# Seven block products for the MLP's up and gate projections, its rows kept in DRAM, and a down projection by halves of the tokens

## The chip, the cores and the metric

The kernel runs on one core of a Trainium2 chip. The metric is device time, in microseconds (us), from one execution to the next run of the same program. The core has five engines, each with its own queue of instructions: TensorE (PE), VectorE (DVE), ScalarE (ACT), GpSimd (POOL) and SyncE (SP), which here issues the DMA transfers. Engines wait for each other through semaphores. PE's operands come from the on-chip memory SBUF and its sums go to the small memory PSUM.

## What is computed

The reference is one layer of an encoder trunk, for 1024 tokens (S) of width 1024 (D), in float32. The change concerns its last part, the MLP, and the output projection of cross attention just before it:

```python
def conv_glu_ffn(h, w_up, conv_w, conv_b, w_down):
    u = dwconv(h @ w_up, conv_w) + conv_b.astype(h.dtype)   # 3 taps along the tokens
    gate, up = jnp.split(u, 2, axis=-1)                     # 2816 columns each
    return (jax.nn.silu(gate) * up) @ w_down
...
        x = x + cross_attention(rms_norm(x, xa_norm[l]), rms_norm(mem, xa_mem_norm[l]),
                                xa_w_q[l], xa_w_kv[l], xa_w_o[l])
        x = x + conv_glu_ffn(rms_norm(x, ffn_norm[l]), ffn_w_up[l], ffn_conv_w[l], ffn_conv_b[l], ffn_w_down[l])
    return rms_norm(x, final_norm)
```

## The kernel before

**Products in three passes.** Activations lie transposed: 128 features on partitions, tokens along the free axis, eight tiles (KD) for the width. A float32 product is made of three: each operand is split into a high part (fp32r) and the rest, and hi x hi, hi x lo, lo x hi are added in PSUM. `K.split` (L140, L142) makes the two parts: ACT copies to `wh`, then POOL (for weights) or DVE (for activations) subtracts into `wl`. A projection `K.proj` gives 128 output rows for all 1024 tokens: eight 128x128 weight blocks, three passes, two halves of 512 tokens, 48 matmuls of 128x512 (L171). Its sum takes one of two PSUM buffers `pp` of 128x1024. Weights come in two pieces of 128x512 floats (256 KB, tile `wr`), in three buffers.

**Into the MLP.** The eight projections of `wo` add to the residual X, which stays in SBUF as eight tiles of 128x1024. `K.residual` applies the norm's gain and splits into `hf` (tile `big`). The norm's factor of each token (`rrow`) is not applied there; it multiplies the projections' results. Its sum over features is a set of small fp32 matmuls (L229 `colsum`, L221 `rows`).

**The MLP.** `ffn` has 22 tiles f of 128 gate rows and 128 up rows. For each f it runs two projections (96 matmuls); DVE takes each out of PSUM times `rrow` (`ut`, L1396), ACT (L203) and DVE (L189, two steps) do the convolution into `c0` and `c1`, ACT the silu (L1398), DVE the product, and ACT and DVE split it into `g`. After every group of four f, `down` (L1412) multiplies the group before it by the down weights: for each of the eight output tiles up to 96 matmuls, added to X. The last two f are done by halves of the tokens (`part`, L1424), so that the first half's final norm runs beside the second half's matmuls.

**What sets the order.** PE's order is that of the program. The other engines' orders are set by a scheduler from the program's dependences, but for DVE's in `part`, which is written out. A tile's buffer is free for its next writer once all readers of the whole tile before are done.

## Time and profile before

| what | us |
|---|---|
| median of three runs | 2501.03 (2498.71 to 2503.26) |
| span of the profiled execution, first to last instruction | 2497.7 |
| PE busy, sum over the span | 2405.6 |
| first matmul of the up projections starts | 1752.86 |
| last matmul of all starts | 2477.64 |

The profile gives, for one execution, what each engine did and when. "Busy" is time in an instruction; a wait is idle time, put down to the instruction that released it. The chain of waits starts at the last instruction and goes back, at each step, to what the instruction waited for; what lies on it sets the time. The granted clock is the share of 2.4 GHz at which PE was allowed to run.

### The profile page before, as it was taken

What the parts mean: (1) busy time and instruction counts of PE and PEld (TensorE: products, weight loads), DVE (VectorE), ACT (ScalarE), POOL (GpSimd) and SP (SyncE); (2) the same over time, 40 slices, a digit from 0 to 9 for tenths busy, and PEclk for the clock granted to TensorE, in tenths of its full rate; (3) what the DMA queues carried; (4) which work ended last, traced back from release to release, by engine and by line L of the source; (5) the groups of instructions that cost most, each with busy time, mean ns of one, the idle gap of its engine ahead of it and who ended that gap; (6) DMA issues with size and microseconds to landing.
All of it is one profiled execution on the core that took longest, in us unless ns stands there. A gap on an engine that the chain in (4) does not pass through costs nothing.

```text
span 2497.7 us, 31082 instructions
## 1 busy us (share of the span) xinstructions
PE 2405.6 (96%) x11750; PEld 1967.1 (79%) x11750; DVE 1397.0 (56%) x2752; ACT 817.4 (33%) x1201; POOL 733.6 (29%) x515
## 2 busy tenths in 40 slices
PE   7999988999999999999999999999999999999997
PEld 6777667778877778786878888888888888888885
DVE  6883998835938658476445633363444243424345
ACT  6362435534224223241231232253333131313123
POOL 6422224525225233241122222202222222222223
PEclk9999999999999999998999999999999999999998
DMA  7443112432111211112264452121111111111112
GB/s 261 112 108 99 38 59 79 129 122 73 61 47 52 72 51 63 48 51 68 86 251 145 134 168 93 43 81 47 47 47 51 47 51 47 51 47 51 47 47 98
DMA packets 112870, 204.25 MB, mean 82 GB/s; under 512 B 12752, under 2 KB 40400, under 8 KB 112592
## 3 DMA queue, kind: packets, MB, share of 16 engines
q1 hardware_dynamic: 112720, 202.26, 24.5%
q8 instruction: 93, 1.52, 0.3%
q14 instruction: 57, 0.47, 0.1%
HBM read 158.17 MB, written 41.94 MB: 80 GB/s over the span
## 4 chain that ended last, share of the span: by engine, by line
PE 72%; DVE 5%; ACT 1%; DMA 1%; POOL 0%; issue 0%; DVEq 0%; SPq 0%; ACTq 0%
PE pp L171 55%; PE pp L1412 9%; PE sm L1105 3%; DVE w L189 1%; PE sm L1315 1%; DVE y L192 1%; PE pp L1424 1%; DVE rb L1031 1%; DVE t L192 1%; PE sm L1047 1%; PE sm L229 0%; PE sm L1061 0%; PE sm L904 0%; PE sm L1092 0%; PE sm L1076 0%; DMA yraw<-yd 0%
## 5 line engine op out<-in xcount | busy, mean ns | idle before, releaser
L171 PE MATMUL pp<-big,wh 128*128 128x512 f32 x3968 | 1105.6, 398 | 16.2 <-DVE sa L192 12.5
L142 POOL TENSOR_TENSOR wl<-wr,wh 128x512 fp32r<-128x512 f32 (+1 forms) x385 | 536.7, 1397 | 1526.2 <-ACT wh L140 1381.5
L171 PEld LDWEIGHTS pp<-big,wh 128*128 128x128 f32 x3968 | 738.7, 190 | 173.7 <-DVE sa L192 14.8
L140 ACT ACTIVATE wh<-wr 128x512 fp32r<-128x512 f32 (+1 forms) x404 | 250.1, 622 | 1213.9 <-PE pp L171 759.3
L171 PE MATMUL pp<-big,wl 128*128 128x512 f32 x1984 | 623.5, 396 | 0.0
L171 PEld LDWEIGHTS pp<-big,wl 128*128 128x128 f32 x1984 | 370.0, 189 | 75.4
L192 DVE TENSOR_TENSOR X<-X,pp 128x1024 f32<-128x1024 f32 (+1 forms) x72 | 79.2, 1101 | 229.3 <-PE pp L1412 129.7
L1412 PE MATMUL pp<-g,wh 128*128 128x512 f32 x640 | 171.0, 389 | 0.0
L192 DVE TENSOR_TENSOR ut<-pp,rrow 128x1024 f32<-128x1024 f32 x44 | 53.9, 1224 | 203.1 <-PE pp L171 199.2
L189 DVE SCALAR_TENSOR_TENSOR c<-ut,vec,c 128x1023 f32<-128x1023 f32 x88 | 113.0, 1284 | 60.6 <-ACT c L203 59.0
L171 PE MATMUL pp<-yhl,wh 128*128 128x512 f32 x512 | 137.4, 390 | 3.3 <-DVE acc L189 2.1
L1412 PEld LDWEIGHTS pp<-g,wh 128*128 128x128 f32 x640 | 120.2, 188 | 24.9
L171 PE MATMUL pp<-bigq,wh 128*128 128x512 f32 x512 | 137.6, 390 | 0.0
L171 PEld LDWEIGHTS pp<-yhl,wh 128*128 128x128 f32 x512 | 95.9, 188 | 24.4 <-DVE acc L189 2.5
L171 PEld LDWEIGHTS pp<-bigq,wh 128*128 128x128 f32 x512 | 95.9, 188 | 20.7 <-DVE bigq L192 0.4
L1412 PE MATMUL pp<-g,wl 128*128 128x512 f32 x320 | 98.5, 389 | 0.0
L171 PE MATMUL pp<-bigq,wl 128*128 128x512 f32 x256 | 78.9, 389 | 0.0
L171 PE MATMUL pp<-yhl,wl 128*128 128x512 f32 x256 | 78.8, 389 | 0.0
L192 DVE TENSOR_TENSOR y<-y,t 128x8 f32<-128x8 f32 (+30 forms) x248 | 77.9, 353 | 0.0
L192 DVE TENSOR_TENSOR t<-rb,x 128x8 f32<-128x8 f32 (+30 forms) x248 | 77.6, 351 | 0.0
L203 ACT ACTIVATE c<-ut,vec 128x1024 f32<-128x1024 f32 x44 | 54.7, 1244 | 46.9 <-DVE ut L192 46.9
L1412 PEld LDWEIGHTS pp<-g,wl 128*128 128x128 f32 x320 | 60.1, 188 | 12.5
(369 smaller groups left out, 2952.1 us busy)
## 6 DMA issues: line engine op xcount, KB each, us to landing
wr<-in_wi SPq DMA_DIRECT2D x144, 256.0 KB, 2.8
wr<-in_wup SPq DMA_DIRECT2D x88, 256.0 KB, 2.7
thd<-tho SPq DMA_DIRECT2D x32, 512.0 KB, 2.9
thi<-thd SPq DMA_DIRECT2D x32, 512.0 KB, 4.0
wr<-in_wdn SPq DMA_DIRECT2D x40, 256.0 KB, 2.6
wr<-in_wkv SPq DMA_DIRECT2D x32, 256.0 KB, 3.6
X<-in_x SPq DMA_DIRECT2D x16, 512.0 KB, 5.3
wr<-in_wbr SPq DMA_DIRECT2D x32, 256.0 KB, 2.8
```

Of the source, the lines that this page charges most:

```text
L140: self.nc.scalar.activation(hi, src, AF.Copy)
L142: e.tensor_tensor(lo, src, hi.bitcast(F32), SUB)
L171: self.nc.tensor.matmul(ps[:, o:o + step], w[:, i], r[:, k, o:o + step], start=first, stop=last)
L189: self.nc.vector.scalar_tensor_tensor(out, in0, s, in1, op0, op1)
L192: (eng or self.nc.vector).tensor_tensor(out, a, b, op)
L203: self.nc.scalar.activation(out, src, AF.Identity, bias=bias, scale=taps[:, left:left + 1])
L1031: nc.vector.stream_shuffle(rb[:, u, s], y[:, u, s], [j] * 32)
L1047: nc.tensor.matmul(p1[:, i], E[:, i, 0:64], y[:, i], start=True, stop=True)
L1105: mm = lambda out, a, b: nc.tensor.matmul(out, a, b, start=True, stop=True)
L1315: nc.tensor.matmul(ps, qt[:, x, d, c], kT[:, y, d], start=k == 0 and i == 0, stop=k == 1 and i == 2)
L1412: nc.tensor.matmul(ps[:, o:o + 512], w[:, i], g[:, x, o:o + 512], start=i == 0 and q == 0, stop=i == n - 1 and q == 2)
L1424: nc.tensor.matmul(ps, w[:, i], g[:, x, c], start=i == 0 and k == 0, stop=i == n - 1 and k == 2)
```

## The change

**Seven products.** For each f the gate and up blocks (two row blocks) by the two halves of the width (A11, A12, A21, A22) are multiplied with the two halves of the width by the two halves of the tokens (B11 to B22). Instead of eight block products of 12 matmuls (128x512 each) there are seven, with sums of blocks as operands (class `Seven`). The sums on the right, B12-B11 and so on, are made once, beside the `wo` projections, and split into seven operands of four tiles: three in `big`, four in the new tiles t0 to t3. The sums on the left are four DVE operations per f; seven pieces are split per f instead of four. The seven results are combined when they are read from PSUM: product 0 to `p1` (ACT), 1 to `u2`, 3 to `u3`, and 2, 4, 5, 6 to the four quarters of the two `ut` tiles (`ready`), where the row factor is applied on DVE or, for all of ut1, on POOL. Products 0 to 3 and 5 take the halves a and b of one `pp` buffer in turn, 4 and 6 half of the other.

**Room for it.** X no longer stays in SBUF: each tile is read, added to, and stored to DRAM (`x2d`). The right operands need a common scale, so they take the factor of the norm before (`rrow` of attention), and its reciprocal is kept (`rcol`) to undo it. The MLP's product goes to DRAM as well (`gd`).

**Down by halves.** `down` starts after the last f: for each half of the tokens the 22 tiles are read back and split into a ring of 24 slots, which the seven operands held before; output tiles go in pairs, each with all 22 f (132 matmuls), so the weights are loaded twice. X comes back from `x2d` at the end of a pair.

```diff
+class Seven:
...
+    def weights(self, s0, s1, m=4):
...
+        a11 = load(s0[:, 0:m])
+        yield self.parts(a11, m)
+        a21, a22 = load(s1[:, 0:m]), load(s1[:, m:2 * m])
+        x1, x2 = self.raw(m), self.raw(m)
+        K.tt(x1, a21, a22, ADD)
+        K.tt(x2, x1, a11, SUB)
+        yield self.parts(x2, m)
+        a12 = load(s0[:, m:2 * m])
+        yield self.parts(a12, m)
+        K.tt(a21, a11, a21, SUB)
+        yield self.parts(a21, m)
+        yield self.parts(x1, m)
+        yield self.parts(a22, m)
+        K.tt(x2, a12, x2, SUB)
+        yield self.parts(x2, m)
...
+    def run(self, s0, s1, x, pool, ready, m=4):
...
+        ab = K.pp.tile([P, S], F32, name="pp")
+        a, b = ab[:, 0:512], ab[:, 512:S]
+        c = None
+        sm = lambda n: pool[n].tile([P, 512], F32, name=n)
+        for n, ps in enumerate((a, b, a, b, c, b, c)):
+            if n == 4:
+                c = K.pp.tile([P, S], F32, name="pp")[:, 0:512]
+            ps = c if ps is None else ps
+            K.run(self.product(ps, next(w), lambda i: x[n][i], n in (0, 1, 4)))
+            if n == 0:
+                p1 = sm("p1")
+                nc.scalar.activation(p1, a, AF.Copy)
+            elif n == 1:
+                u2 = sm("u2")
+                K.tt(u2, b, p1, ADD)
+            elif n == 2:
+                yield
+                ready(0, 0, a, None)
+                continue
+            elif n == 3:
+                u3 = sm("u3")
+                K.tt(u3, b, p1, ADD)
+            elif n == 4:
+                ready(1, 1, c, u3)
+            elif n == 5:
+                ready(1, 0, b, p1)
+            else:
+                ready(0, 1, c, u2)
+            yield
...
+def ffn(K, tc, big, bq, ot, keep, rrow, rcol, x1d, out):
...
+    for j in (0, 4, 1, 5, 2, 6, 3, 7):
+        x = xr.tile([P, S], F32, name="X")
+        nc.sync.dma_start(x, x1d[j])
+        ps = K.run(K.proj(a["wo"][j], ot[:, 0], ot[:, 1]))
+        K.tt(x, x, ps, ADD)
+        nc.sync.dma_start(x2d[j], x)
+        K.stt(g32[:, j], x, K.v("ffnn", j), rrow, MUL, MUL)
+        K.sumsq(xr, x, S, acc)
...
+    for f in range(NFF):
+        def ready(i, h, ps, add):
+            t, c = ts[i], slice(512 * h, 512 * h + 512)
+            if add is None:
+                K.tt(t[:, c], ps, box["row"][:, c], MUL)
+                return
+            K.tt(t[:, c], ps, add, ADD)
+            if i == 0:
+                K.tt(t[:, c], t[:, c], box["row"][:, c], MUL)
+            elif h == 0:
+                K.tt(t, t, box["row"], MUL, nc.gpsimd)
...
+        nc.scalar.activation(c[0], c[0], AF.Silu)
+        K.tt(c[0], c[0], c[1], MUL)
+        nc.sync.dma_start(gd[f], c[0])
...
+    ff.__exit__(None, None, None)
+    fd = right.enter_context(tc.tile_pool(name="fd", bufs=3, side="right"))
+    more = [K.wp, fd] * 3
+    down(K, gp, fd, gd, x2d, ring, X, more, out)
...
+def down(K, gp, fd, gd, x2d, ring, X, pools, out):
...
+        for j0 in range(0, KD, 2):
+            ps = K.pp.tile([P, S], F32, name="pp")
+            w = 0
+            for f0 in range(0, NFF, 4):
+                n = min(4, NFF - f0)
+                ws = []
+                for j in (j0, j0 + 1):
+                    ws.append(K.weights(a["wdn"][j][:, f0:f0 + n], n, pools[w % len(pools)])[0]())
+                    w += 1
...
+                x = X[q][:, j]
+                nc.sync.dma_start(x, x2d[j, :, c])
+                K.tt(x, x, ps[:, 512 * b:512 * b + 512], ADD)
```

On PE, where one projection ends and the next begins in the up stretch, before (`pp_14754` and `pp_14820` are two buffers):

```order
L171 MATMUL pp_14754<-big_13488,wh_14786 128x512 x4
L171 MATMUL pp_14754<-big_13488,wl_14787 128x512 x2
L171 MATMUL pp_14820<-big_13488,wh_14822 128x512 [waits DVE_49,Activation_49]
L171 MATMUL pp_14820<-big_13488,wh_14822 128x512 x3
L171 MATMUL pp_14820<-big_13488,wl_14823 128x512 [waits Pool_49]
```

And now, from product 0 to product 1 of an f (both in `pp_14924`, halves a and b):

```order
L1433 MATMUL pp_14924<-big_13497,wh_14927 128x512 x2
L1433 MATMUL pp_14924<-big_13497,wl_14928 128x512
L1433 MATMUL pp_14924<-big_13497,wh_14953 128x512 [waits Activation_49]
L1433 MATMUL pp_14924<-big_13497,wh_14953 128x512
L1433 MATMUL pp_14924<-big_13497,wl_14954 128x512 [waits Pool_49]
```

The first matmul of product 1 waits for ACT, with the copy of product 0 out of the same buffer; before, the wait at that place was for the buffer two projections back.

On ACT, in the same stretch, before (`wh` are weight splits):

```order
L140 ACTIVATE g_14610<-c0_14474 128x1024
L140 ACTIVATE wh_14756<-wr_14755 128x512
L203 ACTIVATE c0_14613<-ut_14676,vec_71 128x1024
L140 ACTIVATE wh_14786<-wr_14785 128x512
L1398 ACTIVATE c0_14613<-c0_14613 128x1024
L140 ACTIVATE wh_14822<-wr_14821 128x512
L203 ACTIVATE c1_14614<-ut_14742,vec_71 128x1024
L140 ACTIVATE wh_14852<-wr_14851 128x512
```

And now, from the end of one f (`c1_14914`, `c0_14913`) to the copy `p1_14943` of the next:

```order
L140 ACTIVATE wh_14993<-wr_14945 128x512 [waits PE_49,Pool_49]
L140 ACTIVATE wh_15012<-wr_14949 128x512 [waits PE_49,Pool_49]
L203 ACTIVATE c1_14914<-ut_14819,vec_71 128x1024 [waits Pool_49]
L203 ACTIVATE c0_14913<-ut_14818,vec_71 128x1024 [waits DMAHW6_49,DVE_49]
L140 ACTIVATE wh_15029<-wr_14947 128x512 [waits DMAHW4_49,PE_49,Activation_49]
L1453 ACTIVATE p1_14943<-pp_14924 128x512 [waits PE_49]
L1565 ACTIVATE c0_14913<-c0_14913 128x1024 [waits DVE_49,Activation_49]
L140 ACTIVATE wh_15048<-wr_14950 128x512 [waits PE_49]
```

The two convolutions of one f, the second of them behind the first, now stand ahead of the copy that PE's product 1 waits for; the first waits for POOL.

On DVE, before, around one product c0 x c1:

```order
L192 TENSOR_TENSOR ut_14742<-pp_14681,rrow_14111 128x1024
L189 SCALAR_TENSOR_TENSOR c1_14614<-ut_14742,vec_71,c1_14614 128x1023 x2
L192 TENSOR_TENSOR c0_14613<-c0_14613,c1_14614 128x1024
L142 TENSOR_TENSOR g_14749<-c0_14613,g_14749 128x1024
L192 TENSOR_TENSOR ut_14815<-pp_14754,rrow_14111 128x1024
L189 SCALAR_TENSOR_TENSOR c0_14752<-ut_14815,vec_71,c0_14752 128x1023 x2
L192 TENSOR_TENSOR ut_14881<-pp_14820,rrow_14111 128x1024
```

And now, from the second half of ut0 of one f to product 2 of the next:

```order
L192 TENSOR_TENSOR ut_14818<-pp_14858,u2_14816 128x512 [waits PE_49]
L192 TENSOR_TENSOR ut_14818<-ut_14818,rrow_14190 128x512 [waits DVE_49]
L189 SCALAR_TENSOR_TENSOR c1_14914<-ut_14819,vec_71,c1_14914 128x1023 [waits Activation_49]
L189 SCALAR_TENSOR_TENSOR c0_14913<-ut_14818,vec_71,c0_14913 128x1023 [waits DMAHW6_49,Activation_49]
L189 SCALAR_TENSOR_TENSOR c1_14914<-ut_14819,vec_71,c1_14914 128x1023 [waits DVE_49]
L189 SCALAR_TENSOR_TENSOR c0_14913<-ut_14818,vec_71,c0_14913 128x1023 [waits DVE_49]
L192 TENSOR_TENSOR c0_14913<-c0_14913,c1_14914 128x1024 [waits Activation_49]
L192 TENSOR_TENSOR u2_14969<-pp_14924,p1_14943 128x512 [waits PE_49]
L192 TENSOR_TENSOR ut_14971<-pp_14924,rrow_14190 128x512 [waits PE_49]
```

The convolution steps and here also the gate product, which waits for the silu, stand ahead of `u2_14969`, which PE's product 2 waits for; in 11 of the 21 passages `u2` comes ahead of the gate product.

On SP, where the up projections began to give way to down weights, before:

```order
L152 DMA wr_15063<-in_wup 128x512
L152 DMA wr_15099<-in_wup 128x512
L152 DMA wr_15129<-in_wup 128x512
L152 DMA wr_15169<-in_wdn 128x512
L152 DMA wr_15201<-in_wdn 128x512
```

And now, at the end of the last f (`c0_17514`):

```order
L1626 DMA t1_17525<-x2d_13492 128x512 x4
L1626 DMA t2_17526<-x2d_13492 128x512 x8
L1567 DMA gd_13493<-c0_17514 128x1024
L1602 DMA gr_17615<-gd_13493 128x512
L152 DMA wr_17626<-in_wdn 128x512
L152 DMA wr_17662<-in_wdn 128x512
L152 DMA wr_17698<-in_wdn 128x512
L1602 DMA gr_18478<-gd_13493 128x512
```

The weights `wr_17626` for the second output tile of the first pair stand behind the store of the last f's product and its read back. Their space is that of `c0`, `c1` and `ut`.

## Rows read from the trace of the kernel before

**Rows 1.** The page: busy us (share of the span) xinstructions.

```profile
PE 2405.6 (96%) x11750; PEld 1967.1 (79%) x11750; DVE 1397.0 (56%) x2752; ACT 817.4 (33%) x1201; POOL 733.6 (29%) x515
```

**Rows 2.** Chain of waits, MLP: start us, length us, engine, tile, line, count.

```profile
1767.42 163.25 PE pp L171 x720
...
1974.19 87.04 PE pp L171 x384
```

**Rows 3.** Windows: us, each engine's busy us (x instructions), PEclk, DMA share, GB/s.

```profile
1900.00:2100.00 200.00, 200.00 (x884) 165.68 (x883) 76.00 (x61) 48.72 (x60) 49.22 (x37) 1.00 0.16 49
```

**Rows 4.** Groups by form, 1740 to 2478: xcount, busy us, mean ns, idle.

```profile
L192 DVE TENSOR_TENSOR ut<-pp,rrow 128x1024 f32<-128x1024 f32 x44 | 53.9, 1224 | 203.1 <-PE pp L171 199.2 <-ACT rrow L278 3.9
L189 DVE SCALAR_TENSOR_TENSOR c<-ut,vec,c 128x1023 f32<-128x1023 f32 x88 | 113.0, 1284 | 60.6 <-ACT c L203 59.0
L192 DVE TENSOR_TENSOR X<-X,pp 128x512 f32<-128x512 f32 x15 | 10.1, 681 | 3.4 <-PE pp L1424 3.3
L140 ACT ACTIVATE wh<-wr 128x512 fp32r<-128x512 f32 x128 | 80.9, 632 | 443.0 <-PE pp L171 206.1 <-PE pp L1412 154.2 <-issue 82.8
L203 ACT ACTIVATE c<-ut,vec 128x1024 f32<-128x1024 f32 x44 | 54.7, 1244 | 46.9 <-DVE ut L192 46.9
L1398 ACT ACTIVATE c<-c 128x1024 f32<-128x1024 f32 x22 | 23.1, 1048 | 0.0
L142 POOL TENSOR_TENSOR wl<-wr,wh 128x512 fp32r<-128x512 f32 x128 | 175.1, 1368 | 521.9 <-ACT wh L140 521.9
```

**Rows 5.** Groups by form on POOL, whole span: products of 128x1024.

```profile
L142 POOL TENSOR_TENSOR H<-cm,H 128x1024 fp32r<-128x1024 f32 x4 | 11.2, 2798 | 14.7 <-ACT H L140 14.5
L192 POOL TENSOR_TENSOR Bn<-gcr,g_gh 128x1024 fp32r<-128x1024 f32 x4 | 7.6, 1897 | 5.8 <-PE sm L1076 3.8 <-DVE gcr L825 2.1
```

**Rows 6.** Timeline near the end: start us, length us, engine, instruction, [idle <-releaser].

```profile
2455.54 0.40 PE L1424 MATMUL pp<-g,wl 128*128 128x512 f32 x1
2455.98 0.69 DVE L192 TENSOR_TENSOR X<-X,pp 128x512 f32<-128x512 f32 x1 [0.99 <-PE pp L1424]
...
2467.02 0.69 DVE L192 TENSOR_TENSOR sqa<-sqa,hn 128x512 f32<-128x512 f32 x1 [0.70 <-ACT hn L1429]
2467.77 0.97 PEld L229 LDWEIGHTS sm<-ones,sqa 128*128 128x128 f32 x8 [0.90 <-DVE sqa L192]
```

**Rows 7.** Timeline, one POOL operation beside one of DVE.

```profile
1783.56 1.23 DVE L192 TENSOR_TENSOR c<-c,c 128x1024 f32<-128x1024 f32 x1
...
1784.13 1.82 POOL L142 TENSOR_TENSOR wl<-wr,wh 128x512 fp32r<-128x512 f32 x1 [4.14 <-ACT wh L140]
```

**Rows 8.** Timeline of PE after idle time, and windows that follow such restarts.

```profile
296.92 2.08 PE L171 MATMUL pp<-big,wh 128*128 128x512 f32 x4 [4.42 <-DVE sa L192]
485.63 0.73 PE L171 MATMUL pp<-big,wh 128*128 128x512 f32 x2 [1.79 <-DVE sb L192]
1266.86 1.21 PE L171 MATMUL pp<-yhl,wh 128*128 128x512 f32 x4 [2.11 <-DVE acc L189]
...
296.90:302.00 5.10, 5.08 (x12) 4.06 (x13) 4.75 (x15) 4.63 (x4) 0.00 (x0) 0.50 0.00 0
486.00:491.00 5.00, 5.00 (x16) 3.93 (x15) 2.03 (x2) 2.90 (x4) 3.54 (x2) 0.66 0.28 53
1267.00:1272.00 5.00, 5.00 (x22) 4.10 (x23) 2.89 (x2) 0.43 (x1) 1.30 (x1) 1.00 0.91 320
```

**Rows 9.** The page: DMA issues, count, KB each, median us to landing.

```profile
wr<-in_wup SPq DMA_DIRECT2D x88, 256.0 KB, 2.7
thd<-tho SPq DMA_DIRECT2D x32, 512.0 KB, 2.9
thi<-thd SPq DMA_DIRECT2D x32, 512.0 KB, 4.0
```

**Rows 10.** Timeline: the last matmul of all.

```profile
2477.64 0.39 PE L1424 MATMUL pp<-g,wl 128*128 128x512 f32 x1
```

**Rows 11.** Timeline: the first matmuls of the up projections.

```profile
1752.86 1.07 PE L171 MATMUL pp<-big,wh 128*128 128x512 f32 x4
```

More of the change, by code (lines that the diff above doesn't have):

```diff
@@ L209, in conv, with rows @@
                 self.stt(out[:, :n - s], src[:, s:], taps[:, j:j + 1], out[:, :n - s], MUL, ADD)
-    def rows(self, pool, col, nt, gp=False):
-        dg = pool.tile([P, 8, P], F32, name="dg", bufs=1)[:, :nt]
-        self.tt(dg, self.ident.unsqueeze(1).to_broadcast([P, nt, P]), col.unsqueeze(2).to_broadcast([P, nt, P]), MUL,
-                self.nc.gpsimd if gp else None)
+    def rows(self, pool, col, nt, name="dg"):
+        dg = pool.tile([P, max(nt, 4), P], F32, name=name, bufs=1)[:, :nt]
+        self.tt(dg, self.ident.unsqueeze(1).to_broadcast([P, nt, P]), col.unsqueeze(2).to_broadcast([P, nt, P]), MUL)
         f = dg.rearrange("p a b -> p (a b)")
@@ L270, in gained, with rrow @@
         self.sumsq(pool, x, x.shape[-1], accs)
-    def rrow(self, pool, keep, acc, n=S):
+    def rrow(self, pool, keep, acc, n=S, over=None):
         r = self.rstd(pool, self.colsum(acc, n // P), 1.0 / D, EPS)
+        if over is not None:
+            self.nc.vector.reciprocal(over, r)
         yield
@@ L1279, in memory, with queries @@
         yield
-def queries(K, xr, hx, qt, acc, ahead):
-    rr = K.rrow(xr, xr, acc)
+def queries(K, xr, hx, qt, acc, ahead, keep, rcol):
+    rr = K.rrow(xr, keep, acc, over=rcol)
     row = None
@@ L1299, in queries @@
         K.split(qt[:, 0, i], qt[:, 1, i], t, "dve")
+    return row
 UNITS = [(h, t) for h in range(4) for t in range(8)]
@@ new lines, with __init__, raw, parts @@
+class Seven:
+    def __init__(self, K, raws, sets):
+        self.K, self.raws, self.sets = K, raws, sets
+        self.n = [0, 0]
+    def raw(self, m):
+        self.n[0] += 1
+        pool = self.raws[self.n[0] % len(self.raws)]
+        return pool.tile([P, 4, P], F32, name="wr", bufs=3)[:, :m]
+    def parts(self, src, m):
+        self.n[1] += 1
+        pool = self.sets[self.n[1] % len(self.sets)]
+        n = self.sets.count(pool)
+        wh = pool.tile([P, 4, P], F32R, name="wh", bufs=n)[:, :m]
+        wl = pool.tile([P, 4, P], F32R, name="wl", bufs=n)[:, :m]
+        self.K.split(wh, wl, src, "pool")
+        return wh, wl
+    def weights(self, s0, s1, m=4):
+        K = self.K
+        def load(s):
+            t = self.raw(m)
+            K.nc.sync.dma_start(t, s)
+            return t
+        a11 = load(s0[:, 0:m])
[13 more added lines that the diff above has]
+        yield self.parts(x2, m)
+    def product(self, ps, w, x, first):
+        wh, wl = w
+        m = wh.shape[1]
+        for i in range(m):
+            xh, xl = x(i)
+            for j, (a, b) in enumerate(((wh, xh), (wh, xl), (wl, xh))):
+                self.K.nc.tensor.matmul(ps, a[:, i], b, start=first and i == 0 and j == 0,
+                                         stop=i == m - 1 and j == 2, skip_group_check=not first)
+            yield
+    def run(self, s0, s1, x, pool, ready, m=4):
+        K, nc = self.K, self.K.nc
+        w = self.weights(s0, s1, m)
+        ab = K.pp.tile([P, S], F32, name="pp")
[26 more added lines that the diff above has]
+                ready(0, 1, c, u2)
+            yield
@@ L1525, in tile_trunk @@
     x1d = K.dram.tile([KD, P, S], F32, name="x1d")
-    right = ExitStack()
-    with tc.tile_pool(name="bq", bufs=1) as bq:
+    bs = ExitStack()
+    with tc.tile_pool(name="keep", bufs=1, side="right") as keep:
+        bq = bs.enter_context(tc.tile_pool(name="bq", bufs=1))
+        rcol = keep.tile([P, 8], F32, name="rcol")
         with tc.tile_pool(name="at", bufs=1) as at:
@@ L1544, in tile_trunk @@
                 es = {}
-                queries(K, xr, hx, qt, acc[0], lambda: es.update({n: scores(K, at, qt, kT, n) for n in range(AHEAD)}))
+                rrow = queries(K, xr, hx, qt, acc[0],
+                               lambda: es.update({n: scores(K, at, qt, kT, n) for n in range(AHEAD)}), keep, rcol)
             with tc.tile_pool(name="att", bufs=1) as p:
@@ L1548, in tile_trunk @@
                 attend(K, p, at, qt, ot, kT, vt, es)
-        xr = right.enter_context(tc.tile_pool(name="xr2", bufs=1, side="right"))
-        X = xr.tile([P, KD, S], F32, name="X")
-        hf = big.tile([P, 2, KD, S], F32R, name="big")
-        acc = []
-        for j in range(KD):
-            nc.sync.dma_start(X[:, j], x1d[j])
-            ps = K.run(K.proj(a["wo"][j], ot[:, 0], ot[:, 1]))
-            K.residual(xr, X[:, j], ps, j, "ffnn", hf[:, 0], hf[:, 1], acc)
-    ffn(K, X, hf, acc[0], xr, out)
-    right.close()
+        ffn(K, tc, big, bs, ot, keep, rrow, rcol, x1d, out)
 def kernel(**inputs):
```

196 lines of the change are left out of this document (113 added, 83 removed).

## The prediction

> **What bounds the kernel now.** I read the page first: TensorE (PE) is busy 96% of the span [rows 1]. The chain of waits then tells how it runs through the MLP: stretches of hundreds of matmuls with nothing between them [rows 2]. 163.25 / 720 and 87.04 / 384 both give 0.2267 us from one matmul to the next. One f (one pair of 128 gate and 128 up rows) is 96 of them, 21.76 us. The windows over this stretch show PE 100% busy at granted clock 1.00, VectorE (DVE) 38% and ScalarE (ACT) 24% [rows 3]. So matmuls taken out are time gained there, as long as whatever replaces them keeps PE fed.
>
> **What is removed.** Seven products of 12 matmuls are 84 instead of 96 per f: 12 x 0.2267 x 22 = 59.8 us less if PE stays full, 19.04 us per f. The down projection keeps its 1056 matmuls (239.4 us).
>
> **What is added, as totals.** Per f, from [rows 4]: DVE had two ut multiplies and a g split of the same shape (1.22), four convolution steps (1.28) and the gate product (1.23, [rows 7]): 10.0 us. It now has eleven operations of 512 (0.68, the X row): six out of PSUM, one multiply by the row factor, four weight combinations; with the same steps and product 13.9. ACT goes from some 7 to 8.6 (seven wh and p1 at 0.63, two convolutions at 1.24, silu 1.05). GpSimd (POOL) goes from four wl (1.37) to seven plus the multiply of ut1 by the row, 128x1024. The trace has that shape on POOL at 1.90 to 2.80 [rows 5]; two whole operands are nearest the upper row, so 2.8, 12.4 in all. No engine reaches 19 us: totals bound nothing. Waits decide.
>
> **The waits, which are the main term.** Halves a and b of one PSUM tile take products 0, 1, 2, 3 and 5. The order shows a wait on the first matmul of products 1, 2 and 3 of every f: product 1 into b waits for ACT's copy p1 out of a; 2 for u2 (DVE, out of b); 3 for ut0's first half (DVE, out of a). Before, a projection wrote one of two buffers and its eviction ran beside the next 48 matmuls. Now three evictions per f stand between products. A bare one is read at the last projections: the last matmul starts at 2455.54, DVE reads at 2455.98, 0.69 long [rows 6], and PE follows about 0.1 after it (2467.02 + 0.69 to 2467.77). So the next start is 0.44 + 0.68 + 0.1 = 1.2 us after the last start instead of 0.23: a bubble of 1.0.
>
> Two of the three are not bare, as they queue behind the previous f's tail. Take 0 at the start of that f's last matmul and no disturbance. POOL's multiply of ut1 by the row stands behind the wl of the next f's product 3, which waits for product 5 to give its buffers back; that wl ends at -0.4, the multiply at 2.4. ACT has, in this order, convolution 1 (waits for POOL), convolution 0, a wh, p1: 2.4 + 0.1 + 1.24 + 1.24 + 0.63 + 0.63 = 6.2. Product 0 of the new f ended its starts at 2.7, so PE waits and product 1 starts at 6.3, its last matmul at 8.8. DVE's four convolution steps run 3.7 to 8.9. In 11 of the 21 passages from one f to the next u2 comes next (ends 9.9, product 2 starts at 10.0); in the other 10 the gate product stands ahead of u2 and waits for silu (8.9 to 10.0, product to 11.2, u2 to 11.9, start 12.0). Then one bare bubble before product 3, and four products back to back: the last matmul starts at 24.4 or 26.4. So 11 x 24.4 + 10 x 26.4 = 532 us for 21 periods, 25.3 each, where 19.04 was wanted and 21.76 stood.
>
> Two things stretch it. First, POOL's multiply runs beside DVE's multiply of ut0 by the row and a weight combination, both with two operands in SBUF. The trace has one such meeting: a wl that overlaps the c product takes 1.82 instead of 1.37 [rows 7]. That is +0.5 for one, up to +1.2 for both: product 1 starts at 6.8 to 7.5. The Trainium skill, "SBUF — State Buffer", Who interferes with whom, has the two share a port that is held for a whole instruction; by it the multiply would be pushed back by all of both, 1.4 us (2 x 0.68); product 1 would start at 7.7 and, at 0.7 more per period than at 7.0, the sum would be 15 us longer. The 1.82 row, +0.45 for an overlap of 0.66, neither proves nor excludes it.
>
> Second, the clock. Product 0's last matmul ends at 3.1, so PE stands idle 3.2 us undisturbed and 3.7 to 4.4 with POOL held. In [rows 8] PE idle for 4.42 us comes back at granted clock 0.50 (1.2 GHz) for at least 5.1 us; idle for 2.11 it stays at 1.00 (2.4 GHz), and once it fell after 1.79 (0.66 over five us). With product 1 at 7.0 and 0.47 per matmul (the 2.08 for four there), its last matmul starts near 12.1, u2 ends at 13.4 in both kinds of passage, product 2 starts at 13.5, and the period is 27.9. A shorter fall gives 26.9; no fall with POOL held, 26.1. I take 27.0: 21 x 27.0 = 567.
>
> **The ends of the MLP.** *Start.* The eight output projections keep their pace of 48 x 0.2267 = 10.9 us: the splits and subtractions that DVE now has beside one are at most 7 x 0.68 = 4.8 us, and X goes through one buffer, add 1.2, store 2.9, load 4.0 (the same size in [rows 9]), 8.1; without that cover some us each. Then f = 0: from wo's last start, DVE works through the X add, two splits, the gain multiply, eight splits and a subtraction before the sum of squares is complete (about 12). The fp32 column sum takes 1, product 1 waits for the last split of its operand (17), the row factor's matmuls for DVE and POOL (22.8); the next weights land 2.7 later in the space so freed, are split, and five products follow: the last start comes at about 41. *To down.* The weights' second buffer of the first pair lies in space that c0, c1 and ut hold. After the last up matmul: ut0 and its row 1.8, convolutions and steps 7.7, silu 8.8, product 10.2, store landed 13.1, weights 2.7, the last g half and then the weights split on ACT 1.3: PE resumes at 17.3 instead of at 0.2 (only three matmuls come earlier). This I could be wrong on by 5 either way, with DMA queues that I can't see. *Down.* 1053 matmuls, 238.7; the restart at the low clock 2 (some 5 us at 0.50, as after 296.92, lose 2.5, less what is spent waiting anyway); the first half's norm factor 4 (fp32 matmuls and their waits): 17.3 + 238.7 + 6 = 262. *Tail.* Last matmul to the end was 2497.7 - 2477.6 = 20.1 [rows 10]; with 0.4 to 0.6 less of X work, 19.5.
>
> **The sum.** The first up matmul of before starts at 1752.86 of the profiled span [rows 11], wo's last 0.23 earlier, at 1752.6. 1752.6 + 41 + 567 + 262 + 19.5 = 2642.1. The span before was 2497.7 and the median 2501.0, so +3.3: **2645.4**, 5.8% slower.
>
> **Rivals.** (a) *The clock stays up and POOL isn't held.* The period is the undisturbed 25.3: 1752.6 + 41 + 532 + 260 + 19.5 + 3.3 = 2608.4. For it: 3.2 us of idle lies between the rows that fell and those that didn't. Against it: POOL's operation meets two DVE ones in every period. The Trainium skill, "TensorE: Matmul & The Clock Gate", Loop structure matters more than you think, has a loop whose results DVE copies out between dense chains keep its clock; by that this is the case. No row here shows such a loop, since before the evictions made no gap. (b) *Only bare evictions.* If the scheduler's order leaves p1 and u2 free (a conv that runs earlier than I lay it, a POOL multiply of 1.9), each wait costs 1.0 to 1.2: 19.04 + 3.2 = 22.2 per f. 1752.6 + 41 + 21 x 22.2 + 262 + 19.5 + 3.3 = 2544.6. Against it: the queue order is fixed, and the ACT chain has four steps ahead of p1. (c) *The other side: the waits are over when PE gets there.* If the releaser of product 1 were already done (p1 within the 0.2 us between two matmuls) PE runs at 19.04 per f: 1752.6 + 41 + 21 x 19.1 + 262 + 19.5 + 3.3 = 2479.5, faster by 0.9%. The sum is 2078.4 + 21 periods, so it equals the 2501.0 of before at a period of 20.1: the three evictions must cost under 1.1 us per f together, and one bare bubble is 1.0. (d) *The work isn't saved.* The built program has 1848 matmuls where 2112 stood, so no.
>
> **How the numbers follow.** The forecast (serialised, with p1 behind the convolutions and the clock falling in most periods; 26.1 to 28.3 per period, ends off by 8 either way, so 2615 to 2685) has 0.67. (a), 2590 to 2615: 0.18. (b), 2530 to 2580: 0.08. (c): 0.04. Worse than 2690 (falls that last longer, a held DMA queue): 0.03. The range takes the forecast, (a) and the near edge of (b), 2570 to 2690, and leaves out about 0.15. A measurement of this kernel tells 0.2% (5 us) from no change. Faster 0.04, which is (c); within 0.2% 0.01, between (b) and (c); slower 0.95.
>
> **What the profile after would show.** Right: in the up stretch PE near 70% busy; PE's waits name ACT's p1 (about 3 to 4 us each, 21 times), DVE's u2 (1 to 3) and ut (1); a period near 27; the granted clock under 1.00 between products 1 and 2; one wait of some 17 us on the weights' split before the down stretch; the down matmuls still at 0.2267. Clock 1.00 all through and 25.3: (a). Waits of about 1 us alone: (b). A PE at 100% would refute all of it: then halves of a tile would not have to wait for each other, or the queues would run in another order than they stand.

## The result, and the profile after

| what | us |
|---|---|
| median after, 4 runs | 2663.02 (2659.99 to 2669.47) |
| median before, same chip | 2499.87 |
| ratio | 1.0658, 95% interval 1.0641 to 1.0675 |
| profiled execution after, and its span | 2659.99, 2658.2 |

The changed kernel is 6.6% slower. The forecast was 2645.4 with a range of 2570 to 2690: the sign and the size were right and the time lies in the range; the forecast is 17.6 us (0.7%) short of it.

The page after: busy time of each engine, and from the chain of waits the shares by engine and by line. PE does 264 matmuls fewer (11486 against 11750, [rows 1]) and is busy 91% of a longer span.

```profile
PE 2417.1 (91%) x11486; PEld 1942.7 (73%) x11486; DVE 1580.6 (59%) x2983; ACT 901.1 (34%) x1367; POOL 934.3 (35%) x638
...
PE 61%; DVE 13%; ACT 3%; issue 2%; POOL 1%; DMA 1%; SPq 0%; POOLq 0%; DVEq 0%; ACTq 0%
```

PE's waits: engine and tile, what was waited for, total us, times, longest. L1433 are the seven products, L1619 the down projection. Before, this stretch had none of them. Now there are three per f (products 1, 2 and 3), and one at the passage to down.

```profile
PE pp L1433 <- ACT p L1453: 69.9, 21, 3.4
PE pp L1433 <- DVE u L192: 37.0, 21, 5.4
PE pp L1433 <- DVE ut L192: 18.1, 23, 0.9
PE pp L1619 <- DMA wr<-in_wdn: 15.4, 1, 15.4
```

Windows (columns as in [rows 3]) over the steady up stretch, and over 3.4 us after one of the waits: PE is 79% busy where it was 100%, its mean granted clock is 0.92 where it was 1.00, and the second window stands at 0.50, which is 1.2 GHz.

```profile
1800.00:2370.00 570.00, 448.35 (x1726) 344.37 (x1727) 363.63 (x343) 181.53 (x246) 254.17 (x164) 0.92 0.19 65
2213.00:2216.40 3.40, 3.40 (x9) 2.62 (x10) 3.40 (x3) 0.00 (x0) 1.25 (x1) 0.50 0.21 77
```

One passage from an f to the next, from the timeline, without most matmuls. The last matmul of product 6 starts at 2180.90; call that 0. The next matmuls are product 0 of the new f.

```profile
2174.93 0.69 DVE L192 TENSOR_TENSOR wr<-wr 128x512 f32<-128x512 f32 x1 [1.12 <-POOL wl L142]
...
2180.42 2.40 POOL L192 TENSOR_TENSOR ut<-ut,rrow 128x1024 f32<-128x1024 f32 x1
2180.49 2.87 DVE L192 TENSOR_TENSOR wr<-wr 128x512 f32<-128x512 f32 x1 [1.19 <-POOL wl L142]
2180.90 0.39 PE L1433 MATMUL pp<-big,wl 128*128 128x512 f32 x1
...
2182.85 1.25 ACT L203 ACTIVATE c<-ut,vec 128x1024 f32<-128x1024 f32 x1 [1.05 <-POOL ut L192]
2183.29 0.68 DVE L192 TENSOR_TENSOR ut<-pp,u 128x512 f32<-128x512 f32 x1
2184.00 1.06 DVE L192 TENSOR_TENSOR ut<-ut,rrow 128x512 f32<-128x512 f32 x1
2184.98 6.09 DVE L189 SCALAR_TENSOR_TENSOR c<-ut,vec,c 128x1023 f32<-128x1023 f32 x4
2185.09 1.24 ACT L203 ACTIVATE c<-ut,vec 128x1024 f32<-128x1024 f32 x1 [0.99 <-DVE ut L192]
2186.24 0.61 ACT L140 ACTIVATE wh<-wr 128x512 fp32r<-128x512 f32 x1
2186.76 0.57 ACT L1453 ACTIVATE p<-pp 128x512 f32<-128x512 f32 x1
2186.98 1.81 POOL L142 TENSOR_TENSOR wl<-wr,wh 128x512 fp32r<-128x512 f32 x1 [2.48 <-ACT wh L140]
2187.39 0.74 PE L1433 MATMUL pp<-big,wh 128*128 128x512 f32 x2 [3.37 <-ACT p L1453]
...
2190.99 0.68 DVE L192 TENSOR_TENSOR u<-pp,p 128x512 f32<-128x512 f32 x1
```

The reader is to see who holds whom. The weight combination `wr` takes 0.69 alone at 2174.93; at 2180.49, 0.07 us behind the start of POOL's multiply, it takes 2.87. So DVE reaches ut0's last quarter only at 2183.29 (2.4 instead of some 0.4 after the last start), convolution 0 on ACT waits another 0.99 for it, and with `wh` and `p` behind it product 1 starts at 6.49. Then the four steps take 6.09 instead of the 5.1 of [rows 4], u2 ends at 10.8, and product 2 follows. Three of the four take 1.27 to 1.28 as before. The third, which begins while POOL's `wl` of 2186.98 runs, takes 2.31:

```profile
2187.57 2.31 DVE L189 SCALAR_TENSOR_TENSOR c<-ut,vec,c 128x1023 f32<-128x1023 f32 x1
```

The same in the groups by form over the up stretch (1800 to 2370; count, busy us, mean ns, idle before): steps 1547 where they were 1284 [rows 4], combinations 1230, POOL's multiply 2401. The 1547 is a mean of two kinds: over the whole up stretch the 22 steps that begin while a `wl` of POOL runs take 2.3 us, the other 66 take 1.28.

```profile
L189 DVE SCALAR_TENSOR_TENSOR c<-ut,vec,c 128x1023 f32<-128x1023 f32 x84 | 126.6, 1547 | 2.3
L192 DVE TENSOR_TENSOR wr<-wr 128x512 f32<-128x512 f32 x77 | 94.7, 1230 | 62.7 <-POOL wl L142 62.0
L192 POOL TENSOR_TENSOR ut<-ut,rrow 128x1024 f32<-128x1024 f32 x20 | 48.0, 2401 | 0.0
```

Four matmuls that bound the stretches, from PE's timeline: the last of f = 0, the last of the up stretch, the one at which PE resumes in down, the last of all.

```profile
1795.07 0.39 PE L1433 MATMUL pp<-big,wl 128*128 128x512 f32 x1
...
2376.86 0.40 PE L1433 MATMUL pp<-big,wl 128*128 128x512 f32 x1
...
2393.36 1.19 PE L1619 MATMUL pp<-t,wh 128*128 128x512 f32 x2 [15.41 <-DMA wr<-in_wdn]
...
2641.19 0.40 PE L1619 MATMUL pp<-t,wl 128*128 128x512 f32 x1
```

So 21 periods take 2376.86 - 1795.07 = 581.8, 27.7 each, where 19.04 was the cost of 84 matmuls and 21.76 that of 96.

### The profile page after: what moved, and what is told of

The parts are those of the page before. It is cut to its first block, busy times and chain, and to the rows that moved or that the text cites. A ratio compares the mean times of both kernels' runs of the same rounds, so it can differ in the third digit from the quotient of the medians.

```text
span 2658.2 us, 31671 instructions
## 1 busy us (share of the span) xinstructions
PE 2417.1 (91%) x11486; PEld 1942.7 (73%) x11486; DVE 1580.6 (59%) x2983; ACT 901.1 (34%) x1367; POOL 934.3 (35%) x638
## 4 chain that ended last, share of the span: by engine, by line
PE 61%; DVE 13%; ACT 3%; issue 2%; POOL 1%; DMA 1%; SPq 0%; POOLq 0%; DVEq 0%; ACTq 0%
PE pp L171 34%; PE pp L1433 11%; PE pp L1619 9%; DVE c L189 3%; PE sm L1107 3%; DVE wr L192 2%; DVE ut L192 2%; POOL wl L142 1%; DVE w L189 1%; PE sm L1318 1%; ACT c L203 1%; ACT wh L140 1%; DVE t L192 1%; DVE rb L1033 1%; DVE c L192 1%
## 5 line engine op out<-in xcount | busy, mean ns | idle before, releaser
L142 POOL TENSOR_TENSOR wl<-wr,wh 128x512 fp32r<-128x512 f32 x491 | 693.9, 1420 | 1468.6 <-ACT wh L140 1310.8
L171 PE MATMUL pp<-big,wh 128*128 128x512 f32 x2560 | 726.6, 402 | 16.2 <-DVE sa L192 12.5
L140 ACT ACTIVATE wh<-wr 128x512 fp32r<-128x512 f32 (+1 forms) x510 | 316.2, 623 | 1216.3 <-PE pp L171 560.4
L171 PEld LDWEIGHTS pp<-big,wh 128*128 128x128 f32 x2560 | 472.7, 190 | 117.7 <-DVE sa L192 14.8
L171 PE MATMUL pp<-big,wl 128*128 128x512 f32 x1280 | 405.5, 398 | 0.0
L1433 PE MATMUL pp<-big,wh 128*128 128x512 f32 x704 | 253.1, 444 | 111.5 <-ACT p L1453 69.9
L171 PEld LDWEIGHTS pp<-big,wl 128*128 128x128 f32 x1280 | 237.1, 190 | 47.8
L1433 PEld LDWEIGHTS pp<-big,wh 128*128 128x128 f32 x704 | 146.8, 214 | 164.5 <-ACT p L1453 78.9
L1433 PE MATMUL pp<-t,wh 128*128 128x512 f32 x528 | 166.1, 396 | 17.3 <-DVE ut L192 17.3
L1433 PE MATMUL pp<-big,wl 128*128 128x512 f32 x352 | 153.5, 436 | 0.6 <-POOL wl L142 0.6
L192 DVE TENSOR_TENSOR wr<-wr 128x512 f32<-128x512 f32 x88 | 106.6, 1213 | 71.3 <-POOL wl L142 65.4
L1619 PE MATMUL pp<-big,wh 128*128 128x512 f32 x448 | 140.8, 395 | 0.0
L189 DVE SCALAR_TENSOR_TENSOR c<-ut,vec,c 128x1023 f32<-128x1023 f32 x88 | 131.6, 1535 | 2.4
L1433 PEld LDWEIGHTS pp<-t,wh 128*128 128x128 f32 x528 | 97.4, 188 | 46.8 <-DVE ut L192 25.7
L171 PEld LDWEIGHTS pp<-yhl,wh 128*128 128x128 f32 x512 | 95.9, 188 | 24.3 <-DVE acc L189 2.4
L1433 PE MATMUL pp<-t,wl 128*128 128x512 f32 x264 | 103.0, 390 | 0.0
L1619 PEld LDWEIGHTS pp<-big,wh 128*128 128x128 f32 x448 | 84.0, 188 | 20.4 <-issue 0.5
L1619 PE MATMUL pp<-t,wh 128*128 128x512 f32 x256 | 81.5, 400 | 15.4 <-DMA wr<-in_wdn 15.4
```

The costliest lines, as they stand in the source:

```text
L140: self.nc.scalar.activation(hi, src, AF.Copy)
L142: e.tensor_tensor(lo, src, hi.bitcast(F32), SUB)
L171: self.nc.tensor.matmul(ps[:, o:o + step], w[:, i], r[:, k, o:o + step], start=first, stop=last)
L189: self.nc.vector.scalar_tensor_tensor(out, in0, s, in1, op0, op1)
L192: (eng or self.nc.vector).tensor_tensor(out, a, b, op)
L1433: self.K.nc.tensor.matmul(ps, a[:, i], b, start=first and i == 0 and j == 0, stop=i == m - 1 and j == 2, skip_group_check=not first)
```

## The experiments

The theory: the loss is made of (1) waits that exist because a and b are halves of one tile, (2) the order in which DVE, ACT and POOL reach the readings, (3) operations of DVE held by POOL's, and (4) falls of the clock that the waits cause. The rivals put more of it on one of these alone. Ratios are against the kernel before, run on the same chip.

**1. Two tiles instead of two halves.** The order of the products, and which of them share a place, stay as they are.

```diff
-        ab = K.pp.tile([P, S], F32, name="pp")
-        a, b = ab[:, 0:512], ab[:, 512:S]
+        a, b = [K.sm.tile([P, 512], F32, name="sm") for _ in range(2)]
```

> The changed kernel, with the two halves a and b of products 0, 1, 2, 3, 5 in two PSUM tiles of their own instead of halves of one tile; nothing else. Theory (reads of one half hold writes of the other): product 1 no longer waits for p1. What is left is true: product 2 adds into a and waits for p1 (start at 6.5 us after the previous f's last matmul start, where it would be due at 5.7), product 3 waits for u2 (about 9.4 where due at 9.2). Period 20.1 to 20.8 us instead of 27.6, clock 1.00 through the up stretch, total 2510 to 2530. Rival (p1 and u2 are late by their queues, whatever tile holds them, and PE waits as long for them): period above 25, total above 2600.

Measured: 2544.19 us, ratio 1.0182 (1.0163 to 1.0202). The granted clock is 1.00 from 1850 to 2200, the steady period 21.35. PE's waits:

```profile
PE sm L1433 <- DVE u L192: 23.5, 22, 4.7
PE sm L1433 <- ACT p L1452: 8.1, 19, 0.6
```

p's waits fall from 69.9 to 8.1 us (now ahead of product 2) and ut's are gone: product 1 no longer waits for the copy of the other half, though that copy still comes 5.6 to 5.8 after the last start in all passages but two, where it came at 5.8 before. 119 of the 163 us lost are back. Not all of that is the tile's alone: the scheduler, given the two tiles, also put u2 ahead of the gate product in all 21 passages, where it was so in 11, and the clock fell in three periods instead of 16. The five periods of the changed kernel with u2 first and no fall, 25.45, against 21.35 here give 4.1 us per period, some 86 us, for the tile with order and clock alike. The period is above the expected one because u3 before product 5 was not in the reckoning: it queues behind a `wr` held by POOL, and PE waits for it in each f:

```profile
2098.75 1.60 POOL L142 TENSOR_TENSOR wl<-wr,wh 128x512 fp32r<-128x512 f32 x1 [0.81 <-ACT wh L140]
2099.12 1.79 DVE L192 TENSOR_TENSOR wr<-wr 128x512 f32<-128x512 f32 x1
2100.83 0.68 DVE L192 TENSOR_TENSOR u<-sm,p 128x512 f32<-128x512 f32 x1
2101.56 0.74 PE L1433 MATMUL sm<-t,wh 128*128 128x512 f32 x2 [0.59 <-DVE u L192]
```

**2. The longest wait filled.** Twelve matmuls more behind product 0, into a tile of their own; no result is used.

```diff
+            if n == 0 and fill:
+                d = K.sm.tile([P, 512], F32, name="sm")
+                for i in range(fill):
+                    nc.tensor.matmul(d, x[0][0][0][:, 0:P], x[0][0][0], start=i == 0, stop=i == fill - 1)
```

> The changed kernel plus 12 matmuls per f (f = 1 to 21) that nothing reads, into a spare PSUM tile, put behind product 0, where PE waits 3.7 us from start to start; they use operands that are ready, so they delay nothing that PE does next. Theory: the granted clock stays at 1.00, and the passages in which u2 comes ahead of the gate product take 25.4 instead of 26.3 to 27.4, those behind the gate product 27.8 instead of 27.8 to 29.4, as their end is set by DVE: 15 to 21 us less, total 2640 to 2650. Rival (each slow matmul lengthens the time): the matmuls of the up stretch lose 43 us by the clock, so total near 2620. Rival (the clock is not the gap's doing): no change, 2663.

Measured: 2622.89 us, ratio 1.0498 (1.0479 to 1.0517), below the theory and near the rival. No fall in the steady stretch, and every period but the last (30.7) is 25.4 to 25.5. This run alone doesn't decide: the scheduler, seeing a busier PE, also set u2 ahead of the gate product in all passages, where it was so in 11 of 21. Order and clock changed together, so experiment 3 keeps the order and opens most of the gap again.

**3. Three matmuls in place of the twelve.** The same kernel with fill=3.

> The filled-gap kernel (twelve extra matmuls of 128x512 behind product 0, 2622.9 us) with three extra matmuls in place of twelve: 0.68 us of the 3.3 us wait is filled, 2.6 stay open. VectorE's order is that of the filled one in nearly all passages (u2 ahead of the gate product), so the order's gain over the changed kernel, about ten passages x 2.2 = 22 us, is here too, and only the idle time differs. Theory (the clock falls after idle times of this size): the granted clock falls again in a good part of the periods, those being 26.2 to 26.5 instead of 25.4; total 2632 to 2643. Rival (the filled kernel's gain was the order's alone, or an idle time of 2.6 is too short for a fall): no falls, 25.4 throughout, 2620 to 2626.

Measured: 2635.41 us, ratio 1.055 (1.0533 to 1.0566). Windows from 1850 to 2200, first experiment 2, then this one:

```profile
1850.00:2200.00 350.00, 311.47 (x1316) 243.51 (x1315) 239.51 (x223) 116.74 (x154) 168.92 (x110) 1.00 0.20 67
```

```profile
1850.00:2200.00 350.00, 288.91 (x1159) 223.91 (x1158) 237.64 (x217) 112.89 (x150) 165.88 (x107) 0.96 0.19 65
```

In the first twenty passages u2 is ahead in both kernels; the clock falls in 13 of the 20 periods here (3.4 us at 1.2 GHz each) and in none of them there. Periods with a fall are 26.2 to 26.7 and those without 25.4 to 25.5: 13 x 1.1 = 14 us, of which 12.5 show in the medians. So the clock is a cost of its own. The other 27.6 us between the changed kernel and this one go with the order: a gate product ahead of u2 delays u2 by itself, and in the changed kernel all ten such periods also show 6.8 us at the low clock instead of 3.4 or none. In that kernel's trace, behind one fall of 3.4 us u2 ends 11.5 to 11.9 after the last start where it comes first and 13.1 to 13.2 behind the gate product; behind a fall of 6.8 it ends at 12.7 (one period) and again at 13.1 to 13.2. How order and clock share the 27.6 wasn't separated further.

**4. POOL's multiply moved to DVE.**

```diff
-                K.tt(t, t, box["row"], MUL, nc.gpsimd)
+                K.tt(t, t, box["row"], MUL)
```

> The changed kernel with the multiply of ut1 by the row on DVE instead of POOL; nothing else. Theory (POOL's multiply holds DVE for its whole 2.4 us, the weight combination behind it takes 2.87, and ut0, convolution 0, p1 and product 1 follow late; the scheduler now also puts u2 ahead of every gate product): product 1 starts at 4.5 after the previous f's last matmul start instead of 6.5, product 2 at 8.3, the period is 22.6, clock 1.00, total 2550 to 2570. Rival (DVE is the bound and gets 1.2 us more to do): slower than 2663. Rival (ACT's queue of two convolutions and a weight split is what delays p1, whoever multiplies): product 1 at 6 or later, 2640 to 2663.

Measured: 2624.44 us, ratio 1.0504 (1.0487 to 1.0521): 39 us better than the changed kernel, and 55 us above what was expected. One passage of it; the `wr` group from 1850 to 2200 stands last:

```profile
2079.63 0.69 DVE L192 TENSOR_TENSOR ut<-ut,rrow 128x512 f32<-128x512 f32 x1
2080.24 7.13 DVE L189 SCALAR_TENSOR_TENSOR c<-ut,vec,c 128x1023 f32<-128x1023 f32 x4
...
2082.65 0.73 PE L1433 MATMUL pp<-big,wh 128*128 128x512 f32 x2 [1.76 <-ACT p L1453]
...
2088.02 0.73 PE L1433 MATMUL pp<-big,wh 128*128 128x512 f32 x2 [2.34 <-DVE u L192]
```

```profile
L192 DVE TENSOR_TENSOR wr<-wr 128x512 f32<-128x512 f32 x55 | 37.9, 689 | 29.9 <-POOL wl L142 29.4
```

The hold is shown: without POOL's multiply `wr` is 689 ns on the mean, instead of 1230, and the row multiply of ut0 0.69 instead of 1.06. Product 1 came 4.87 after the last start (4.5 was expected). The gain was then given back at product 2 (10.2, not 8.3): the four steps, now early, run beside three `wl` of POOL and take 7.13. The wait went from p (38.0 us in all, from 69.9) to u (47.5, from 37.0). And the clock still fell, 14 times, for 51 us in all: two waits of 1.8 and 2.3 stand close together here.

**5. The down weights in the seven products' own buffers.** The edit takes the space conflict between up and down away: the weights of down use `seven.raw` and `seven.parts`, and the pool of the convolution stays open.

```diff
-    more = [K.wp, fd] * 3
-    down(K, gp, fd, gd, x2d, ring, X, more, out)
+    down(K, gp, fp, fe, gd, x2d, ring, X, seven, out)
...
-                    ws.append(K.weights(a["wdn"][j][:, f0:f0 + n], n, pools[w % len(pools)])[0]())
+                    raw = seven.raw(n)
+                    nc.sync.dma_start(raw, a["wdn"][j][:, f0:f0 + n])
+                    ws.append(seven.parts(raw, n))
```

> The changed kernel with the down projection's weights in the five buffers that the up projection used, instead of in a pool that takes the space of c0, c1 and ut; the small tiles of the norms take those tiles' names. Theory (the wait of 15.8 us between up and down is for space, which is free only when the last f's product is in DRAM): the wait falls to under 3 us, total 2646 to 2652. Rival (the wait is for the last f's product itself, or the DMA queue): the wait stays above 10 us, total 2658 to 2665.

Measured: 2652.53 us, ratio 1.0616 (1.0592 to 1.064), 10.5 better, just above the 2646 to 2652 expected. The 15.4 us wait is gone (down starts 0.23 after the last up matmul), but in the profiled execution up itself ended 12 us later, at 2388.80, with more time at the low clock (116 us of the up stretch against 96), while its three waits per f sum to the same. Why the clock fell more often there wasn't pursued.

**6. An order by hand.** Two tiles, the buffers of experiment 5, and the orders of DVE, ACT and POOL written out: weights prepared four products ahead, the tail of the f before dealt out one or two operations to a product, each reading right behind its product. In the diff `next(pend)` issues one such piece of the f before.

```diff
+    with tc.manual_schedule(engines={mybir.EngineType.DVE, mybir.EngineType.Activation, mybir.EngineType.Pool}):
...
+            if pend:
+                next(pend)
+            K.run(seven.product(ps, ready[k], lambda i: x7[n][i], n in (0, 1, 4)))
...
+            elif n == 3:
+                u3 = fp.tile([P, 512], F32, name="u3")
+                K.tt(u3, ps, p1, ADD)
```

> Halves a and b in two PSUM tiles, the down weights in the up's buffers, and the orders of DVE, ACT and POOL in the up stretch written out: each reading of a product out of PSUM stands right behind that product, and the previous f's convolution, silu and gate product are laid one or two operations at a time into the products that follow; weights are split four products ahead. The same operations as in the changed kernel. Theory (waits and queues, no engine's total, cost the time): period 19.1 to 19.8 us, clock 1.00, no wait between up and down, total 2470 to 2500, so at or under the kernel before. Rival (DVE, held by POOL, is the bound: its operations of one f sum to some 17.5 us at the durations that they had beside POOL): period 20.5 to 21.4, total 2505 to 2530.

Measured: 2490.02 us, ratio 0.9963 (0.995 to 0.9975): barely faster than before. Most periods are 20.0 to 20.4, above the 19.1 to 19.8 expected. One wait is left in the steady stretch, 1.0 from start to start before product 5:

```profile
2004.24 3.94 DVE L189 SCALAR_TENSOR_TENSOR c<-ut,vec,c 128x1023 f32<-128x1023 f32 x2
2008.10 0.68 DVE L192 TENSOR_TENSOR u<-sm,p 128x512 f32<-128x512 f32 x1
...
2008.93 0.70 PE L1433 MATMUL sm<-t,wh 128*128 128x512 f32 x2 [0.67 <-DVE u L192]
```

Two steps, beside POOL's `wl`, stand ahead of u3 and take 3.94, where two of [rows 4] would take 2.6.

**7. The same order on the halves of one tile.** This takes the two tiles of experiment 6 back and leaves all else.

> As the hand-ordered kernel, but with a and b as halves of one PSUM tile as in the changed kernel: only the queues' orders and the down weights' buffers differ from the changed kernel. Theory (three waits for readings that now start at once): 19.04 + 3 x 1.0 = 22.1 us per period, 2540 to 2560 in all. Rival (three short waits per f bring the clock down, as waits of 1.8 and 2.3 us did with the row multiply on DVE): period 23 to 25, 2565 to 2610.

Measured: 2555.34 us, ratio 1.0221 (1.0202 to 1.024). The steady period is 22.4 to 22.6, and there all three waits are bare:

```profile
PE pp L1433 <- DVE u L192: 34.0, 22, 4.7
PE pp L1433 <- DVE ut L192: 17.3, 22, 0.8
PE pp L1433 <- ACT p L1597: 14.4, 21, 0.7
```

Start to start they are 1.24 (u2), 1.17 (ut0) and 1.08 (p), so 0.85 to 1.0 each beyond the usual 0.23: the prediction's bare bubble. The tile's halves cost 65 us with this order (2555.3 against 2490.0). Some 48 of them are 21 times the difference of the steady periods, 22.5 and 20.2 on the mean. Much of the rest lies in periods 2 to 5: there u2 stands behind a split of down's first g, PE waits 3.0 to 4.7 us for it, the clock falls each time, and the periods are 25.9 to 28.7.

**8. One step moved behind u3.** From experiment 6, one step of c1 goes from ahead of u3 to the slot behind it.

```diff
         right_(0)
-        left(1)
         yield                                   # 3
+        left(1)
         nc.scalar.activation(c[0], c[0], AF.Silu)
```

> Against the hand-ordered kernel with two tiles (2490.0 us, most periods 20.15 to 20.25), one convolution step of c1 is moved on VectorE from ahead of u3's reading to the slot behind it, ahead of the reading of product 4. Nothing else changes. Theory: the one wait that is left (before product 5, 1.0 per period, put down to u) exists because two steps (3.94 us, held by POOL's subtraction) stand ahead of u3; with one step there u3 starts when product 3 ends, and the wait goes. Period 19.2 to 19.5, total 2468 to 2478. Rival: VectorE has some 17 us of work per period and the moved step pushes the reading of product 4, so that the wait comes back before product 6 (or as a later gate product and ut row before the next f): period 19.9 to 20.3, total 2483 to 2492.

Measured: 2470.03 us (2468.43 to 2473.89), ratio 0.9891 (0.9874 to 0.9909): 1.1% faster than before, the best of the study. Behind f = 0, periods are 19.25 to 20.04 from one copy p to the next, most of them 19.3; the last, which ends at down's first matmul, is 24.3, with a wait of 2.5 for u3. Now DVE waits for product 3 and not PE for DVE:

```profile
2052.20 1.54 DVE L189 SCALAR_TENSOR_TENSOR c<-ut,vec,c 128x1023 f32<-128x1023 f32 x1
2054.32 0.69 DVE L192 TENSOR_TENSOR u<-sm,p 128x512 f32<-128x512 f32 x1 [0.58 <-PE sm L1433]
```

Five kernels side by side (medians in us):

| | scheduler's order | order by hand | and one step moved |
|---|---|---|---|
| halves of one tile | 2652.5 (buffers as in 5) | 2555.3 | |
| two tiles | 2544.2 (buffers as in the change) | 2490.0 | 2470.0 |

The order alone brings 97 us, the two tiles 119 (from 2663.0, with the change of the scheduler's order that came with them), both together 162 (from 2652.5) and not 216: each of them by itself shortens the same long wait before product 1.

## Why the prediction was right, and where its numbers were off

| term | forecast | profiled execution |
|---|---|---|
| wo's last start | 1752.6 | 1752.2 |
| f = 0, to its last start | 41 | 42.9 |
| 21 periods | 567.0 | 581.8 |
| PE resumes in down, then all of down | 17.3, 262 in all | 16.5, 264.3 in all |
| tail | 19.5 | 17.0 |
| span to metric | 3.3 | 1.8 |

**What was read rightly.** *Three waits per f*: products 1, 2 and 3 wait for p and u 21 times each and for ut 23 times, as the waits show. Experiment 1 shows the reason that was given, one tile with two halves. *Totals bound nothing*: in the up stretch DVE is busy 64% and PE 79%. *The bare bubble of 1.0*, read from the last projections [rows 6], is what experiment 7 measures. *The clock*: it fell in 16 of the 21 periods, as "most" said. *The passage to down*: 16.5 against 17.3. Product 1's start, 6.49 between the 6.3 (undisturbed) and the 6.8 to 7.5 (POOL held) of the forecast, isn't in this list: it came out near by luck, as two errors cancel.

**The step that failed in its working, though not in its sum, is who holds whom: POOL's multiply was to be pushed back by DVE.** The multiply was taken at 2.8 plus 0.5 to 1.2. It takes 2.40 whenever it starts first, and DVE's `wr` beside it waits it out: 2.87 against 0.69, 2.18 us of hold. In [rows 7] DVE had started first and POOL was the slower one; that row was read as a rule on who loses, and it only showed who had come second. Nor was it the trace's one such meeting: 17 of the 22 gate products of before begin ahead of a `wl` and take 1.23, with the `wl` at 1.81; the other five begin behind one and take 1.55, with the `wl` at 1.3. The first of the five:

```profile
1936.45 1.31 POOL L142 TENSOR_TENSOR wl<-wr,wh 128x512 fp32r<-128x512 f32 x1 [4.14 <-ACT wh L140]
1937.28 1.55 DVE L192 TENSOR_TENSOR c<-c,c 128x1024 f32<-128x1024 f32 x1
```

ACT's chain then lost its time at another link: convolution 1 could start at 1.95, earlier than the 2.5 (undisturbed) of the forecast, and convolution 0 waited 0.99 for DVE's ut0, which the forecast had ready. The two errors cancel at product 1. They don't cancel afterwards: the steps begin later and one of the four, behind a `wl`, takes 2.3 where 1.28 was taken from [rows 4]; u2 ends at 10.8 instead of 9.9, and a period of the kind forecast at 24.4 undisturbed (some 25.2 with the 0.8 that the forecast gave to POOL's hold) is 25.45 without any fall of the clock. Experiment 4 shows both holds apart: the first goes with the multiply, the second grows when the steps move.

The Trainium skill, "SBUF — State Buffer", Who interferes with whom, has a DVE instruction with two SBUF inputs contend with a POOL instruction that reads SBUF, and says that issue order decides who blocks. The trace agrees on both: 2.87 for DVE where POOL began 0.07 earlier, 1.82 for POOL where DVE began 0.57 earlier [rows 7]. The prediction cited this section for the length of the hold and passed over its sentence on the order.

**The term that was mis-sized** is the period, 27.0 against 27.7, 14.8 us in all. In the changed kernel's trace the eleven periods with u2 first are 25.4 to 25.5 (five, no fall of the clock), 26.2 to 26.6 (four, 3.4 us at 1.2 GHz), 27.5 (one, 6.8 us) and 32.1 (the last, 6.8 us and a wait of 5.4 for u2, behind splits of down's first g on DVE); the ten with the gate product first are 27.8 to 31.0, all with 6.8 us at the low clock. The forecast had 27.9 for any period with a long fall, from a stretch of at least 5.1 us [rows 8]; here four of the ten have one fall of 6.8 about product 1 (27.8 to 27.9), five have two of 3.4, one behind the wait before product 1 and one behind the longer wait before product 2 (29.4 to 29.5), and the first has its 6.8 behind the wait before product 2 (31.0). The other terms are off by 0.4 to 2.5 each and nearly cancel, and the median lies 3.0 above the profiled execution; f = 0 is 1.9 longer, since product 2 starts at 25.7, where the forecast has its weights land (22.8 + 2.7), but waits 0.6 more for `wl` and stands at 1.2 GHz for most of its matmuls.

**The rivals.** (a), clock up and POOL not held, 25.3 per period: experiment 2 has 25.45 with the clock up, near (a)'s period by accident, since u2 is first in all its passages, for which (a) had 24.4, and DVE is held. Why (a) didn't come is the clock: in 14 of the 21 periods of the changed kernel the idle time of 3.3 before product 1 went with a fall, in two more the longer wait before product 2 did. The Trainium skill, "TensorE: Matmul & The Clock Gate", Loop structure matters more than you think, on which (a) could lean, isn't borne out where PE waits for the copy: the next matmuls do not "follow immediately" here, they come 3.3 us later, and the clock is at 0.50 behind many of them. (b), only bare evictions, 22.2 per f and 2544.6: experiment 7 is this case in its steady period, 22.4 to 22.6; its total, 2555.3, is near by accident in part, as it lacks the wait ahead of down and has four periods with falls. Its condition, an order that leaves p and u2 free, is what the scheduler didn't give. (c), the evictions over when PE gets there, needed under 1.1 us of waits per f to reach the time of before. Experiment 6 has 1.0 us of waits and 2490, experiment 8 some 0.3 and 2470; both also lack the 15 us wait ahead of down, so the point of (c) itself wasn't met by a run. (d) was excluded by the count of instructions, and the page shows 11486.

**The products do save what was promised, where they are fed.** In experiment 8 one f costs 19.3 against 21.76. From the first up matmul to the last matmul the best version takes 697.8 us where [rows 10, 11] give 724.8: 27 of the ideal 59.8; f = 0 (33.6 us from its first p to the next), the slower first periods and the last one (24.3) take most of the rest.

## What to carry to other kernels

When fewer matmuls are bought with more evictions, count the places where PE must wait for an eviction before the next product, and price each from the barest one in the trace (1.0 us here): three of them (2.8 us in experiment 7) are more than the 2.7 us that twelve matmuls are worth, before any queue is counted. Give each product that alternates its own tile, and write the order of the reading engines so that at most one foreign operation stands ahead of a reading. Where POOL and DVE both read two operands from SBUF at once, look at who begins first and add what is left of that one to the other, less some 0.2 us: of the 2.33 left of POOL's multiply `wr` paid 2.18, of the 1.22 left of a `wl` the step paid 1.03, and of the 0.66 left of DVE's gate product [rows 7] the `wl` paid 0.5 (1.82 against 1.3).
